# A two-layer transformer step on one core: written order around the layer norms, statistics in halves, last norm's shift as a two-row product

## The chip, the cores and the metric

One core of a Trainium2 chip. The metric is device time in microseconds (us) from launch to end; lower is better. Three runs of the kernel before gave 2600.35, 2598.08 and 2597.52 us (median 2598.08).

## The reference, cut to what matters

Two layers over 256 tokens (g = 0: 128 prompt tokens, g = 1: 128 latent tokens), width 2048. Each layer norm is followed by an adaLN modulation that feeds the next weight product.

```python
def hybrid_layer(x, mods, ...):
    shift1, scale1, gate1, shift2, scale2, gate2 = mods
    h = modulate(x, shift1, scale1)
    q, k, v, hq, hff, hfb, hi, hgt = split_in(h @ w_in_l)
    ...
    mix = jnp.concatenate([att, hg], -1) @ w_o_l
    x = layer_norm(DEEPNORM_ALPHA * x + gate1 * mix, ln_g_l[0], ln_b_l[0])
    ffn = sq_relu_mlp(modulate(x, shift2, scale2), w_up_l, w_down_l)
    x = layer_norm(DEEPNORM_ALPHA * x + gate2 * ffn, ln_g_l[1], ln_b_l[1])
    return x, k, v, s_f, s_b
```

## The kernel before, in words

**Weight stream.** All weights are read once from HBM, in items of 1 MB (two `raw` tiles of 128x1024 f32), loaded by the queue of SyncE (L1310). Ten `raw` buffers hold five items. A *main* item is a block of w_in, w_o, w_up or w_down: ScalarE rounds it to `wh` (L1328), VectorE forms the remainder `wl` (L1329), and TensorE makes three products per block, hi x wh, lo x wh and hi x wl, where `hh`/`hl` are the rounded activations and their remainder. Kind "T" (L445, L447, L448) has the weights stationary and 256 columns moving; kind "N" (L457 to L459) has the activations stationary and 512 columns moving. Four main items (kg = 0 to 3, two or four per part of w_o) make a *unit* with two PSUM banks (for N: g = 0 and g = 1), which a `done` function empties. A *mod* item is a block of w_mod: either four f32 products with two rows of output each on TensorE (L203), or four multiply-adds on VectorE (L266, tile `ma`).

**Order.** `seq` is the written list of items; `put_unit` lays main items and, by the credits RATE and PRATE, mod items between them; `flush` puts out the mod items that must be done. Waiting tasks (attention, scan, plain norm outputs) are stepped in between by `pump`. The order on SyncE and GpSimd is as written; that on TensorE, VectorE and ScalarE is chosen by a list scheduler when the program is built, except inside `manual_schedule`. Each engine then runs its list in order.

**The norms.** There are four: norm 1 (layer 0, behind w_o), norm 2 (layer 0, behind w_down), norm 3 (layer 1, behind w_o) and norm 4 (layer 1, behind w_down, the output). The unit just ahead of a norm I call its *tail*. `add_gated` or `d_down` multiplies each PSUM bank by the gate `G`, adds it to the residual (`Y` or `Z`) and takes `bn_stats` (L891). For norms 1 to 3 `ln_mod` (L933) then aggregates (L909), forms the reciprocal deviation (L621 to L627, two steps of it on ScalarE), normalises each chunk of 512 columns on VectorE (L942), transposes it on TensorE into `pt` (L947), applies scale and shift by feature (`scale_shift`: g = 0 on VectorE L929, g = 1 on ScalarE L931) into `ed`, and splits the result into `hh` (L408, ScalarE) and `hl` (L409, VectorE). One chunk is the activation of one kg of the next unit. After it, `GAP` = 6 mod items are put in. `ln_out` writes the plain output of the norm (times gamma, plus beta, L1013 and L1014) as a task; its rows of gamma and beta are loaded by GpSimd's queue into the two `G` buffers.

**Norm 4** (`ln_last_ordered`): gamma and beta are loaded for all four chunks; two of the eight tiles are finished on GpSimd, one is shared, five take two VectorE instructions each (L974, L998), and each is stored by SyncE.

## Time and profile before

| what | value |
|---|---|
| median of three runs | 2598.08 us |
| the profiled execution, its own time | 2595.31 us |
| its span, first to last instruction | 2593.4 us |
| mean granted TensorE clock | 0.989 |
| busy: VectorE, ScalarE, GpSimd | 1849.1, 1227.5, 105.0 us |
| moved by DMA | 652.77 MB, 252 GB/s in the mean |

Busy time of TensorE counts each matmul with its drain, so two that follow closely overlap; how fast it works is read from the distance of starts. In a timeline a row gives start, duration, engine, line, operation and, in brackets, the idle time before it with what ended it.

### The profile page before, as it was taken

The page shows a single profiled execution, that of the slowest core. Times are in us where ns is not written, and L with a number is a line of the kernel's source. Part 1 is how long each engine was busy: PE and PEld are TensorE (multiplying, and loading weights), DVE is VectorE, ACT ScalarE, POOL GpSimd, SP SyncE. Part 2 cuts the span into 40 slices and gives each one's busy share as a digit, 9 for nine tenths or more (in the row PEclk, how much of TensorE's full clock was granted, in tenths as well). Part 3 has the DMA queues.
Part 4 walks back from the last instruction along what each step waited for, and adds up shares of the span by engine and source line. Part 5 has one row for each costly group of instructions (what it writes and reads, how often), then busy time and mean ns, then how long its engine had stood idle before and what let it go on. Part 6 is the DMA issues. An engine that isn't in the chain of part 4 may idle for free.

```text
span 2593.4 us, 41149 instructions
## 1 busy us (share of the span) xinstructions
PE 2508.7 (97%) x16276; PEld 2150.2 (83%) x16276; DVE 1849.1 (71%) x2332; ACT 1227.5 (47%) x1703; POOL 105.0 (4%) x188
## 2 busy tenths in 40 slices
PE   7999899999999999999999999999899999999996
PEld 4787777768989879879877989788798998998985
DVE  3455778679887777887777788868865565666656
ACT  3434565435545444444435666744544454443542
POOL 2000000000000000000000010001000000000002
PEclk9999999999999999999999999999999999999998
DMA  9889778989987787887878576566576666666663
GB/s 357 271 285 321 268 246 284 325 277 359 315 295 274 267 292 269 285 276 263 288 234 292 193 243 197 193 221 223 187 235 218 212 215 217 217 200 227 204 206 115
DMA packets 192304, 652.77 MB, mean 252 GB/s; under 512 B 22720, under 2 KB 25344, under 8 KB 192112
## 3 DMA queue, kind: packets, MB, share of 16 engines
q1 hardware_dynamic: 177680, 614.56, 69.1%
q0 software_dynamic: 11488, 32.91, 4.3%
q8 instruction: 127, 2.08, 0.3%
q10 hardware_dynamic: 2944, 2.69, 0.3%
q14 instruction: 65, 0.53, 0.1%
HBM read 643.19 MB, written 6.88 MB: 251 GB/s over the span
## 4 chain that ended last, share of the span: by engine, by line
PE 61%; issue 28%; DMA 5%; DVE 4%; ACT 1%; POOL 0%; SPq 0%; POOLq 0%; DVEq 0%; ACTq 0%
PE acc L445 9%; PE acc L447 9%; PE acc L448 9%; PE acc L457 9%; PE acc L459 9%; PE acc L458 9%; DMA raw<-in_w_mod_dram 2%; PE psm L203 2%; DVE wl L1329 1%; PE psm L223 1%; DMA out_nsf_dram<-lf 1%; PE pI L757 1%; PE pX L780 1%; DMA raw<-in_w_in_dram 0%; PE pO L818 0%
## 5 line engine op out<-in xcount | busy, mean ns | idle before, releaser
L1328 ACT CAST wh<-raw 128x1024 fp32r<-128x1024 f32 x784 | 821.7, 1049 | 1065.3 <-PE acc L459 456.2
L1329 DVE TENSOR_TENSOR wl<-raw,wh 128x1024 fp32r<-128x1024 f32 x784 | 953.6, 1222 | 416.1 <-ACT wh L1328 397.1
L445 PE MATMUL acc<-hh,wh 128*128 128x256 f32 x3072 | 878.4, 286 | 3.0 <-DVE q L608 1.7
L448 PE MATMUL acc<-hh,wl 128*128 128x256 f32 x3072 | 871.3, 284 | 5.5 <-DVE wl L1329 5.5
L447 PE MATMUL acc<-hl,wh 128*128 128x256 f32 x3072 | 871.4, 284 | 0.0
L445 PEld LDWEIGHTS acc<-hh,wh 128*128 128x128 f32 x3072 | 589.9, 192 | 40.9 <-issue 31.2
L448 PEld LDWEIGHTS acc<-hh,wl 128*128 128x128 f32 x3072 | 589.9, 192 | 6.5 <-DVE wl L1329 6.5
L447 PEld LDWEIGHTS acc<-hl,wh 128*128 128x128 f32 x3072 | 590.2, 192 | 0.9 <-issue 0.2
L266 DVE SCALAR_TENSOR_TENSOR ma<-raw,stat,ma 128x1024 f32<-128x1024 f32 x300 | 378.6, 1281 | 95.0 <-DMA raw<-in_w_mod_dram 91.2
L458 PE MATMUL acc<-wl,fh 128*128 128x512 f32 x1024 | 399.4, 390 | 4.7 <-DVE wl L1329 4.7
L457 PE MATMUL acc<-wh,fh 128*128 128x512 f32 x1024 | 400.6, 391 | 1.8 <-DVE Z L1241 1.8
L459 PE MATMUL acc<-wh,fl 128*128 128x512 f32 x1024 | 398.9, 390 | 0.0
L457 PEld LDWEIGHTS acc<-wh,fh 128*128 128x128 f32 x1024 | 192.3, 188 | 51.0 <-issue 7.7
L458 PEld LDWEIGHTS acc<-wl,fh 128*128 128x128 f32 x1024 | 192.3, 188 | 45.4 <-DVE wl L1329 6.3
L459 PEld LDWEIGHTS acc<-wh,fl 128*128 128x128 f32 x1024 | 192.3, 188 | 40.0
L458 PE MATMUL acc<-wl,hh 128*128 128x512 f32 x320 | 129.4, 404 | 4.4 <-DVE wl L1329 4.4
L457 PE MATMUL acc<-wh,hh 128*128 128x512 f32 x320 | 131.3, 412 | 2.1 <-ACT hh L408 2.1
L459 PE MATMUL acc<-wh,hl 128*128 128x512 f32 x320 | 127.8, 402 | 0.0
L457 PE MATMUL acc<-wh,mxh 128*128 128x512 f32 x256 | 103.2, 404 | 0.0
L458 PE MATMUL acc<-wl,mxh 128*128 128x512 f32 x256 | 100.1, 392 | 0.0
L459 PE MATMUL acc<-wh,mxl 128*128 128x512 f32 x256 | 100.0, 392 | 0.0
L203 PE MATMUL psm<-raw,stat 128*2 128x512 f32 x640 | 95.0, 596 | 2.4 <-DMA raw<-in_w_mod_dram 2.4
(360 smaller groups left out, 1902.6 us busy)
## 6 DMA issues: line engine op xcount, KB each, us to landing
raw<-in_w_mod_dram SPq DMA_DIRECT2D x384, 512.0 KB
raw<-in_w_up_dram SPq DMA_DIRECT2D x256, 512.0 KB
raw<-in_w_down_dram SPq DMA_DIRECT2D x256, 512.0 KB
raw<-in_w_in_dram SPq DMA_DIRECT2D x208, 512.0 KB
...
```

What stands on the lines that cost most here:

```text
L203: pe.matmul(self.ps[32 * j:32 * j + 2, :], lhsT=stat[:, k, :], rhs=raw[j // 2][:, 512 * (j % 2):512 * (j % 2) + 512], start=k == 0, stop=k ...
L223: pe.matmul(self.ps[32 * j:32 * j + 2, :], lhsT=stat[:, 4 * k + j, :], rhs=raw[j // 2][:, 512 * (j % 2):512 * (j % 2) + 512], start=k == 0 ...
L266: dve.scalar_tensor_tensor(self.acc[g], raw[h], c, self.acc[g], ALU.mult, ALU.add)
L445: pe.matmul(ps, lhsT=w0, rhs=hi[:, k], start=f and k == 0 and m % 2 == 0, stop=False, skip_group_check=True)
L447: pe.matmul(ps, lhsT=w0, rhs=lo[:, k], start=False, stop=False, skip_group_check=True)
L448: pe.matmul(ps, lhsT=w1, rhs=hi[:, k], start=False, stop=e and k == 3 and m % 2 == 1, skip_group_check=True)
L457: pe.matmul(ps, lhsT=hi[:, k, gs], rhs=wh[k], start=f and k == 0, stop=False)
L458: pe.matmul(ps, lhsT=hi[:, k, gs], rhs=wl[k], start=False, stop=False)
L459: pe.matmul(ps, lhsT=lo[:, k, gs], rhs=wh[k], start=False, stop=e and k == 3)
L757: pe.matmul(pI[:, 128 * m:128 * m + 128], lhsT=ke[:, 128 * m:128 * m + 128], rhs=qe[:, 128 * m:128 * m + 128], start=True, stop=True)
L1328: act.copy(wh, r)
L1329: dve.tensor_tensor(wl, r, wh.bitcast(F32), ALU.subtract)
```

## The change

It does these things:

- In the tail unit the g = 1 half of the last kg runs as two halves of 256 columns (`n_tile` with `cols`), and gate, add and `bn_stats` of g = 1 go by halves.
- From the tail's last main item to the end of the next unit, VectorE and ScalarE run in written order (`ordered`). In it the `wh` of two main items is made ahead of the norm (`split(..., False)`), chunk 0 is normalised on two engines (g = 0 ScalarE, g = 1 VectorE), its `hh` is made on ScalarE straight from PSUM while VectorE makes the unrounded copy, and chunk n + 1 is normalised as part of chunk n. The chunks of `ln_mod` now stand between the main items of the next unit.
- No mod items by RATE within the tail; the `flush` ahead of a norm stands before the tail; GAP goes from 6 to 4, and those items stand behind kg = 1 of the next unit.
- The plain outputs of a norm may not be issued before the last `hl` of `ln_mod` (`issue_after`).
- Norm 4: gamma multiplies chunks 0 to 2 already as they are emptied. Then shift: `-mean*rstd*gamma + beta` is made by TensorE as a product with two rows (gamma and beta of a chunk at partitions 32n) into PSUM, one for each of six tiles; VectorE takes one instruction for each of these and two for each tile of chunk 3. GpSimd computes nothing there. The loads for it are put two units earlier: eight single rows and five broadcasts in place of eight broadcasts.

```diff
+                if g == 1 and un.tail:
+                    for h in range(2):
+                        n_tile(un, g, range(4), hi, lo, wh, wl, f, e, slice(256 * h, 256 * h + 256))
+                else:
+                    n_tile(un, g, range(4), hi, lo, wh, wl, f, e)
...
+    def add_gated(key, n, g, ps, gt, first, last, tail):
+
+        for cols in halves(g) if tail else [slice(0, 512)]:
+            t = gt[:, cols]
+            dve.tensor_tensor(t, ps[:, cols], t, ALU.mult)
+            y = yt[key, n, g][:, cols]
+            if first:
+                dve.scalar_tensor_tensor(y, y, ALPHA, t, ALU.mult, ALU.add)
+            else:
+                dve.tensor_tensor(y, y, t, ALU.add)
+            if last and tail:
+                stats(key, n, g, cols.start // 256)
+        if last and not tail:
+            for h in range(len(halves(g))):
+                stats(key, n, g, h)
...
+    def ln_norm(key, n, g):
+        mr, nb = lnst[key]
+        y = yt[key, n, g]
+        if g == 0:
+            act.activation(y, y, AF.Identity, scale=mr[0][1], bias=nb)
+        else:
+            dve.tensor_scalar(y, y, mr[1][0], mr[1][1], ALU.subtract, ALU.mult)
+
+    def ln_open(key):
         mr = ln_stat(key)
+        nb = small(1)
+        dve.scalar_tensor_tensor(nb, mr[0][0], -1.0, mr[0][1], ALU.mult, ALU.mult)
+        lnst[key] = mr, nb
+        for g in range(2):
+            ln_norm(key, 0, g)
+
+    def ln_mod(key, AB, dst, n):
+
+        A, B = (x[:, 4 * n:4 * n + 4] for x in AB)
+        hl = new_act("h")
+        gs = [slice(0, 128), slice(128, 256)]
+        pt, t = {}, {}
+        for g in (1, 0):
+            pt[g] = bank("pt")
+            t[g] = u("ed")
+            for c in range(4):
+                pe.transpose(pt[g][:, 128 * c:128 * c + 128], yt[key, n, g][:, 128 * c:128 * c + 128], K["ident"])
+        if n == 0:
+            for c in range(4):
+                for g in (1, 0):
+                    act.activation(hl[0][:, c, gs[g]], pt[g][:, 128 * c:128 * c + 128], AF.Identity,
+                                   scale=A[:, c, g:g + 1], bias=B[:, c, g:g + 1])
+            ln_norm(key, 1, 1)
+            for c in range(4):
+                cs = slice(128 * c, 128 * c + 128)
+                for g in (1, 0):
+                    dve.tensor_scalar(t[g][:, cs], pt[g][:, cs], A[:, c, g:g + 1], B[:, c, g:g + 1],
+                                      ALU.mult, ALU.add)
+            ln_norm(key, 1, 0)
+        else:
+            for g in (1, 0):
+                scale_shift(t[g], pt[g], A, B, g)
+            for g in (0, 1):
+                act.copy(hl[0][:, :, gs[g]], v3(t[g], 4))
+            if n < 3:
+                for g in (1, 0):
+                    ln_norm(key, n + 1, g)
+        for g in (0, 1):
+            lnend[key] = dve.tensor_tensor(hl[1][:, :, gs[g]], v3(t[g], 4), hl[0][:, :, gs[g]].bitcast(F32),
+                                           ALU.subtract)
+        dst[n] = hl
...
+    def ordered(on):
+
+        if on:
+            region[0] = tc.manual_schedule(engines={mybir.EngineType.DVE, mybir.EngineType.Activation})
+            region[0].__enter__()
+        else:
+            region[0].__exit__(None, None, None)
...
+                side.dma_start(gb[32 * n + i:32 * n + i + 1, :], a[src][li:li + 1, 512 * n:512 * n + 512])
+        lgb["rows"] = gb
         for n in range(4):
-            tag = ("w", "t", "e1", "ed")[n]
-            gt, bt = u(tag), u(tag)
-            side.dma_start(gt, a["lng"][li:li + 1, 512 * n:512 * n + 512].partition_broadcast(128))
-            side.dma_start(bt, a["lnb"][li:li + 1, 512 * n:512 * n + 512].partition_broadcast(128))
-            lgb[li, n] = (gt, bt)
+            lgb["g", n] = rows(("e1", "e1", "ed", "ed")[n], "lng", n)
+        lgb["b", 3] = rows("w", "lnb", 3)
+        mr = u("t", 256)
+        dve.memset(mr, 0.0)
+        dve.memset(mr.rearrange("p (x r) -> p x r", r=32)[:, :, 1], 1.0)
+        lgb["mr"] = mr
...
+        st = ln_stat(key)
+        mr = lgb["mr"]
         for g in range(2):
+            m, r = st[g]
+            cols = mr[:, 128 * g:128 * g + 128].rearrange("p (n r) -> p n r", r=32)[:, :, 0]
+            dve.scalar_tensor_tensor(cols, m.to_broadcast([128, 4]), -1.0, r.to_broadcast([128, 4]),
+                                     ALU.mult, ALU.mult)
+        pt = bank("pt")
+        for g in range(2):
+            pe.transpose(pt[:, 128 * g:128 * g + 128], mr[:, 128 * g:128 * g + 128], K["ident"])
+        cf = u("t", 256)
+        act.copy(cf, pt[:, 0:256])
+        ps = {}
+        for g in range(2):
+            for n in range(3):
+                ps[n, g] = bank("pz")
+                pe.matmul(ps[n, g], lhsT=cf[32 * n:32 * n + 2, 128 * g:128 * g + 128],
+                          rhs=lgb["rows"][32 * n:32 * n + 2, :], start=True, stop=True, tile_position=(32 * n, 0))
+        for g in range(2):
+            y = ys[3, g]
+            dve.scalar_tensor_tensor(y, y, st[g][0], lgb["g", 3], ALU.subtract, ALU.mult)
+            dve.scalar_tensor_tensor(y, y, st[g][1], lgb["b", 3], ALU.mult, ALU.add)
+            store(3, g)
+        for g in range(2):
+            for n in range(3):
+                y = ys[n, g]
+                dve.scalar_tensor_tensor(y, y, st[g][1], ps[n, g], ALU.mult, ALU.add)
+                store(n, g)
...
+                with tc.issue_after(lnend[key].ins):
+                    dve.tensor_tensor(y, y, gt, ALU.mult)
+                    dve.tensor_tensor(y, y, bt, ALU.add)
...
+        opening = closing = False
+        if norm:
+            key, coef, dst = norm[0][:3]
+            opening, closing = un.tail, not un.tail
         for kg in un.groups:
+            if opening and kg == un.groups[-1]:
+                AB = []
+                put_call(drain)
+                put_call(lambda: AB.append(ln_coef(*coef)))
+                put_call(lambda: ordered(True))
+                norm[0] += (AB,)
+            if closing:
+                AB = norm[0][3]
+                if kg == 0:
+                    put_call(lambda: split(main_ahead(at[0], 2), False))
+                    put_call(lambda: ln_open(key))
+                    put_call(lambda: ln_mod(key, AB[0], dst, 0))
+                if kg == 1:
+                    credit[0] += GAP
+                if kg < 3:
+                    put_call(lambda kg=kg: ln_mod(key, AB[0], dst, kg + 1))
+                else:
+                    norm.pop()
             seq.append(("main", Main(un, kg)))
+            if closing and kg == 3:
+                put_call(lambda: ordered(False))
...
+                tail = part == len(PARTS[l]) - 1 and n == 3
+                if tail:
+                    flush((l, 3), (l, 4))
+                    put_norm(k1, (l, 4, 3, 2 * l), h2)
+                put_unit(Unit("N", lambda kg, n=n: a["w_o"][l, n, kg], getM, d_wo(n, part), gr, tail),
+                         0 if tail else RATE[l, "o"], None,
...
-                        t = macc.pop((n, g))
-                        gt = gch.pop((l, 5, n, g, 0))
-                        dve.tensor_tensor(gt, un.ps[g], gt, ALU.mult)
-                        dve.tensor_tensor(t, t, gt, ALU.add)
-                        yt[k2, n, g] = t
-                        stats(k2, n, g)
+                        yt[k2, n, g] = macc.pop((n, g))
+                        add_gated(k2, n, g, un.ps[g], gch.pop((l, 5, n, g, 0)), False, True, un.tail)
+                        if l == L - 1 and n < 3:
+                            y = yt[k2, n, g]
+                            dve.tensor_tensor(y, y, lgb["g", n], ALU.mult)
...
-                    if l == L - 1 and n == 2:
+                    if l == L - 1 and n == 0:
                         put_call(lambda: load_gb(2 * l + 1))
+                tail = sc == 3 and n == 3
+                if tail and l + 1 < L:
+                    flush((l + 1, 0), (l + 1, 1))
+                    put_norm(k2, (l + 1, 1, 0, 2 * l + 1), hcur)
...
-    GAP = 6
+    GAP = 4
...
+    def split(upto, low=True):
+
         while nsplit[0] < min(upto, len(seq)):
             i = nsplit[0]
             issue(i + 1)
             if nd[0] <= i:
-                return
+                break
             it = seq[i]
             if it[0] == "main":
                 m = it[1]
                 m.wh, m.wl = [], []
                 for r in raws.pop(i):
                     wh = whp.tile([128, 1024], F32R, tag="wh", name=nm("wh"))
-                    wl = wlp.tile([128, 1024], F32R, tag="wl", name=nm("wl"))
                     act.copy(wh, r)
-                    dve.tensor_tensor(wl, r, wh.bitcast(F32), ALU.subtract)
                     m.wh += [wh[:, 0:512], wh[:, 512:1024]]
-                    m.wl += [wl[:, 0:512], wl[:, 512:1024]]
-                live[0] -= 2
+                    lows.append((m, wh, r))
+                if low:
+                    split_low()
             nsplit[0] += 1
+        if low:
+            split_low()
+
+    def split_low():
+        for m, wh, r in lows:
+            wl = wlp.tile([128, 1024], F32R, tag="wl", name=nm("wl"))
+            dve.tensor_tensor(wl, r, wh.bitcast(F32), ALU.subtract)
+            m.wl += [wl[:, 0:512], wl[:, 512:1024]]
+            live[0] -= 1
+        lows.clear()
```

**The order on TensorE around norm 1.** Before, at the end of the tail (`psm` rows are mod items, `pt` rows the transposes of a chunk; each mod row is two of the four products of an item):

```order
L459 MATMUL acc_5558<-wh_5543,mxl_5180 128x512
L203 MATMUL psm_5587<-raw_5483,stat 2x512 x2
L203 MATMUL psm_5587<-raw_5485,stat 2x512 x2
L203 MATMUL psm_5587<-raw_5531,stat 2x512 x2
L203 MATMUL psm_5587<-raw_5533,stat 2x512 x2
L203 MATMUL psm_5587<-raw_5547,stat 2x512 x2
L203 MATMUL psm_5587<-raw_5549,stat 2x512 x2
L203 MATMUL psm_5587<-raw_5593,stat 2x512 x2
L203 MATMUL psm_5587<-raw_5595,stat 2x512 x2
L203 MATMUL psm_5587<-raw_5605,stat 2x512
L947 MATMUL pt_5669<-ident_591,Y_4461 128x128 x4
L947 MATMUL pt_5681<-ident_591,Y_4457 128x128 x4
```

Now, at the same place:

```order
L463 MATMUL acc_5561<-wh_5544,mxh_5179 128x256
L465 MATMUL acc_5561<-wl_5548,mxh_5179 128x256
L466 MATMUL acc_5561<-wh_5544,mxl_5180 128x256
L979 MATMUL pt_5677<-ident_591,Y_4461 128x128 x4
L979 MATMUL pt_5683<-ident_591,Y_4457 128x128 x4
L979 MATMUL pt_5711<-ident_591,Y_4664 128x128 x4
L450 MATMUL acc_5745<-hh_5675,wh_5597 128x256
L450 MATMUL acc_5758<-hh_5675,wh_5597 128x256
L979 MATMUL pt_5717<-ident_591,Y_4660 128x128 x4
L452 MATMUL acc_5745<-hl_5676,wh_5597 128x256
```

The mod items between the tail and the first transposes are gone (before there are 24 of their products, six items, between the tail and the first main product of w_up); 16 transposes in place of 24 stand ahead of the first product that needs `hl`. At norm 2 the list now has 16 mod products in this place in place of 24; at norm 3 there were and are none.

**The order on VectorE at norm 3.** Before, from the tail's g = 0 bank on (`wl` rows belong to the weights of the next unit):

```order
L896 TENSOR_TENSOR G_17825<-acc_17841,G_17825 128x512
L901 TENSOR_TENSOR Y_17458<-Y_17458,G_17825 128x512
L891 BN_STATS bs_17651<-Y_17458 128x6
L909 BN_AGGR s_17914<-bs_17651 128x2
L1329 TENSOR_TENSOR wl_18040<-raw_17707,wh_18039 128x1024
L896 TENSOR_TENSOR G_17827<-acc_17848,G_17827 128x512
L1329 TENSOR_TENSOR wl_18044<-raw_17709,wh_18043 128x1024
L901 TENSOR_TENSOR Y_17462<-Y_17462,G_17827 128x512
L891 BN_STATS bs_17655<-Y_17462 128x6
L909 BN_AGGR s_17914<-bs_17655 128x2
```

Now:

```order
L911 TENSOR_TENSOR G_17866<-acc_17892,G_17866 128x512
L916 TENSOR_TENSOR Y_17472<-Y_17472,G_17866 128x512
L905 BN_STATS bs_17673<-Y_17472 128x6
L911 TENSOR_TENSOR G_17868<-acc_17899,G_17868 128x256
L916 TENSOR_TENSOR Y_17476<-Y_17476,G_17868 128x256
L905 BN_STATS bs_17677<-Y_17476 128x6
L911 TENSOR_TENSOR G_17868<-acc_17899,G_17868 128x256
L916 TENSOR_TENSOR Y_17476<-Y_17476,G_17868 128x256
L905 BN_STATS bs_17677<-Y_17476 128x6
L927 BN_AGGR s_17996<-bs_17673 128x2
L927 BN_AGGR s_17996<-bs_17677 128x2
```

The two `wl` subtractions are no longer among the statistics of g = 1; these go by halves.

**The plain outputs on VectorE behind norm 1** (`Y` rows, times gamma and then plus beta). Before:

```order
L1013 TENSOR_TENSOR Y_4457<-Y_4457,G_6629 128x512
L1013 TENSOR_TENSOR Y_4461<-Y_4461,G_6629 128x512
L1329 TENSOR_TENSOR wl_6160<-raw_6013,wh_6159 128x1024
L1014 TENSOR_TENSOR Y_4457<-Y_4457,G_6630 128x512
L1329 TENSOR_TENSOR wl_6164<-raw_6015,wh_6163 128x1024
L266 SCALAR_TENSOR_TENSOR ma_6007<-raw_6025,stat,ma_6007 128x1024
L266 SCALAR_TENSOR_TENSOR ma_6008<-raw_6025,stat,ma_6008 128x1024
L266 SCALAR_TENSOR_TENSOR ma_6007<-raw_6027,stat,ma_6007 128x1024
L1329 TENSOR_TENSOR wl_6228<-raw_6097,wh_6227 128x1024
L266 SCALAR_TENSOR_TENSOR ma_6008<-raw_6027,stat,ma_6008 128x1024
L1329 TENSOR_TENSOR wl_6232<-raw_6099,wh_6231 128x1024
L1014 TENSOR_TENSOR Y_4461<-Y_4461,G_6630 128x512
```

Now:

```order
L1001 TENSOR_TENSOR hl_5918<-ed_5920,hh_5917 128x4x128
L1091 TENSOR_TENSOR Y_4457<-Y_4457,G_6626 128x512
L1091 TENSOR_TENSOR Y_4461<-Y_4461,G_6626 128x512
L1092 TENSOR_TENSOR Y_4457<-Y_4457,G_6627 128x512
L1092 TENSOR_TENSOR Y_4461<-Y_4461,G_6627 128x512
L1450 TENSOR_TENSOR wl_5947<-raw_5889,wh_5943 128x1024
L1091 TENSOR_TENSOR Y_4660<-Y_4660,G_6986 128x512
L1450 TENSOR_TENSOR wl_5949<-raw_5891,wh_5945 128x1024
```

They now stand directly behind the last `hl`, and the first instruction of the second chunk (`G_6986`, a `G` buffer that has to be loaded again) stands between the two `wl` of kg = 3.

## Rows read from the trace of the kernel before

**Rows 1.** Page of the profile, part 1: busy time of each engine.

```profile
PE 2508.7 (97%) x16276; PEld 2150.2 (83%) x16276; DVE 1849.1 (71%) x2332; ACT 1227.5 (47%) x1703; POOL 105.0 (4%) x188
```

**Rows 2.** Stretches, TensorE: us, busy (instructions), granted clock, DMA share, GB/s.

```profile
600.00:602.00 2.00, 2.00 (x12) 1.00 1.03 410
...
1382.00:1384.00 2.00, 2.00 (x6) 0.53 0.87 277
...
1838.00:1840.00 2.00, 0.00 (x0) 0.88 1.00 391
...
1846.00:1848.00 2.00, 1.70 (x14) 0.92 0.00 0
...
2576.00:2578.00 2.00, 0.00 (x0) 0.70 0.00 0
```

**Rows 3.** Lines of TensorE, 590.7 to 602.4 us: count, busy, mean ns, idle before.

```profile
L203 PE MATMUL psm<-raw,stat 128*2 128x512 f32 x48 | 8.0, 592 | 0.9 <-DMA raw<-in_w_mod_dram 0.9
```

**Rows 4.** Timeline around norm 1, TensorE, VectorE and ScalarE in turn.

```profile
590.52 0.39 PE L459 MATMUL acc<-wh,mxl 128*128 128x512 f32 x1
...
602.46 0.48 PE L445 MATMUL acc<-hh,wh 128*128 128x256 f32 x2
...
608.18 1.03 PE L947 MATMUL pt<-ident,Y 128*128 128x128 f32 x8
608.97 0.36 PE L448 MATMUL acc<-hh,wl 128*128 128x256 f32 x1
609.26 1.04 PE L203 MATMUL psm<-raw,stat 128*2 128x512 f32 x8
610.23 0.39 PE L445 MATMUL acc<-hh,wh 128*128 128x256 f32 x1
...
590.95 0.69 DVE L896 TENSOR_TENSOR G<-acc,G 128x512 f32<-128x512 f32 x1 [0.28 <-PE acc L459]
...
593.43 0.17 DVE L621 TENSOR_SCALAR s<-s 128x2 f32<-128x2 f32 x1
...
594.90 2.37 DVE L942 TENSOR_SCALAR Y<-Y,s,s 128x512 f32<-128x512 f32 x5
...
604.36 1.29 DVE L409 TENSOR_TENSOR hl<-ed,hh 128x512 fp32r<-128x512 f32 x2
...
602.17 1.50 ACT L931 ACTIVATE ed<-pt,B,A 128x128 f32<-128x128 f32 x4
```

**Rows 5.** Timeline around norm 2, TensorE.

```profile
1359.94 0.39 PE L459 MATMUL acc<-wh,fl 128*128 128x512 f32 x1
...
1371.79 0.48 PE L457 MATMUL acc<-wh,hh 128*128 128x512 f32 x1
...
1381.01 0.50 PE L458 MATMUL acc<-wl,hh 128*128 128x512 f32 x1 [2.12 <-DVE wl L1329]
...
1382.81 0.63 PE L459 MATMUL acc<-wh,hl 128*128 128x512 f32 x1
```

**Rows 6.** Timeline around norm 3, TensorE.

```profile
1836.41 0.39 PE L459 MATMUL acc<-wh,mxl 128*128 128x512 f32 x1
...
1849.18 0.36 PE L447 MATMUL acc<-hl,wh 128*128 128x256 f32 x1
```

**Rows 7.** Timeline of norm 4, TensorE and VectorE.

```profile
2571.80 0.39 PE L459 MATMUL acc<-wh,fl 128*128 128x512 f32 x1
...
2577.76 1.64 DVE L998 SCALAR_TENSOR_TENSOR Z<-Z,s,t 128x512 f32<-128x512 f32 x1
...
2588.22 0.75 DVE L998 SCALAR_TENSOR_TENSOR Z<-Z,s,ed 128x512 f32<-128x512 f32 x1
```

**Rows 8.** Line 563, f32 products of 512 columns: durations ns min/median/max.

```profile
L563 PE MATMUL pr<-q,rot x8: 590/592/596, 488.7 to 1769.6; 128*128 128x512 f32 x8
```

**Rows 9.** Timeline behind norm 3, VectorE and TensorE.

```profile
1876.70 0.69 DVE L1013 TENSOR_TENSOR Y<-Y,G 128x512 f32<-128x512 f32 x1 [4.58 <-DMA G<-in_lng_dram]
...
1879.77 0.38 PE L448 MATMUL acc<-hh,wl 128*128 128x256 f32 x1 [1.13 <-DVE wl L1329]
```

119 lines of the change are left out of this document (40 added, 79 removed).

## The prediction

> **What bounds the kernel now.** I read part 1 of the page first: TensorE is busy 97% of the span, VectorE, the next, 71% [rows 1]. So time is lost where TensorE stands still, and an edit counts by the TensorE idle time that it adds or takes away. A mod item is work that must be done somewhere: moved, it costs nothing in itself, but it fills a hole or leaves one open. Next come the stretches, for clock and DMA load at the norms [rows 2], and the lines of TensorE at norm 1 [rows 3]; then the timeline of each norm, from the start M of the tail's last matmul to the first matmul behind it [rows 4 to 7].
>
> At norm 1 M is 590.52 and the first main product 602.46, a gap of 11.94 us. The reader is to see that it isn't empty. Eight mod rows take 0.97, 0.121 each [rows 4], so the 48 of the gap [rows 3] take 5.8; eight transposes take 0.79, 0.1 each [rows 4], and the 24 ahead of the first product that needs `hl` take 2.4. The last matmul itself takes 0.23 (its 0.39 holds a tail of 0.16). Idle: 11.94 - 5.8 - 2.4 - 0.23 = 3.5 us.
>
> Norm 2 has the same work in a gap of 11.85 (1359.94 to 1371.79): 3.4 idle. Behind it TensorE waits 2.1 for a `wl`, and then eight matmuls start 0.43 apart, each 0.63 long, in place of 0.23 apart and 0.39 long, 1.6 lost [rows 5]; the granted clock reads 0.53, near 1.2 GHz [rows 2]. In all 7.1.
>
> Norm 3 has no mod items in its gap, which is 12.77 long (1836.41 to 1849.18) [rows 6]: less 28 transposes (2.8), 0.23 and two short products (0.24), 9.5 idle.
>
> **Norms 1 and 3: the new chain.** VectorE starts 0.43 behind M (590.95) [rows 4]. A gate multiplication of 512 columns takes 0.69 there; for a half I take 0.45, between its half, 0.36 with some fixed cost, and the whole, 0.72. Three such (the last half's gate, add, statistics) are 1.35, and two aggregates 0.6, an estimate from the 2.48 between 590.95 and 593.43, in which three whole operations stand besides. So M + 2.4. From there to the normalisation 1.47 (593.43 to 594.90), plus 0.2 for the new `nb`: M + 4.05. Half a microsecond for a tile (five in 2.37) makes M + 4.6, eight transposes and the way there M + 5.7. Then ScalarE forms `hh` in eight pieces: four took 1.50, so 0.35 each and a longer last one, 2.9, M + 8.7 with the hand-overs. Two `hl` take 1.3 (1.29) [rows 4]: M + 10.1. Near norm 3 the clock reads 0.88 two microseconds behind M and 0.92 when transposes run again [rows 2]; for eight transposes at half clock I add 0.8: M + 10.9. Ends: 9.8 (halves at 0.36, full clock), and 11.7 (halves at 0.72).
>
> In it TensorE has 16 transposes (1.6) and 0.4 of short products, the last matmul among them: 8.9 idle. The lists show it: no mod item stands there any more. **Norm 1: 8.9 - 3.5 = +5.4. Norm 3: 8.9 - 9.5 = -0.6.** The main costs of norm 1 that the change takes away (normalisation of later chunks out of the way, `wh` made ahead) are in the shorter chain already; the six mod items are done before the tail and behind kg = 1, where VectorE and the DMA have other work.
>
> **Norm 2.** Here 16 mod products stand in the gap (32 rows, 3.9), 16 transposes (1.6) and four matmuls (0.9). They keep TensorE at work, so the chain ends at M + 10.1; with 0.1 for the last matmul, 3.6 is idle. The `wl` of two items is made behind the norm now, before its products need it, so I let the 2.1 and the 1.6 go. **3.6 - 7.1 = -3.5**; if both stay, +0.2.
>
> **Plain outputs.** Behind norm 1 the first instruction on the second chunk stands between two `wl` of kg = 3, and needs a `G` buffer that GpSimd's queue loads again. What waits behind it on VectorE is the other `wl`, and behind that TensorE. The nearest rows are behind norm 3: VectorE waited 4.58 for such a load, and 1.13 of it reached TensorE [rows 9]. Between 0 and 4.6; I take **+0.7**, near the lower of the two, since the products of kg = 2 and the mod items stand ahead.
>
> **Norm 4.** M is 2571.80. Before, the last instruction of VectorE ends at 2588.97, M + 17.17, and the span (2593.4) at M + 21.6, 4.43 later for the store. While GpSimd computes, VectorE's instruction takes 1.64, alone 0.75 [rows 7]. Now GpSimd computes nothing. Statistics are done at M + 3.9 (as above without `nb`); chunk 3 takes four instructions and the six other tiles one each: 10 x 0.75 = 7.5, M + 11.4, 5.75 earlier than before, if no product is late. A product is an f32 one of 512 columns in two passes; a pass lasts 0.59 [rows 8] with the tail of 0.16, so 0.43, a product 0.86. Columns, transposes and copy end near M + 5. One after another at full clock, product i is ready at M + 5.2 + 0.86 i, the sixth at M + 10.3, and VectorE wants it at M + 10.65: no wait. At half clock, as the stretch that reads 0.70 in this place suggests [rows 2], the sixth is ready at M + 15.5 and VectorE ends at M + 16.3: only -0.8. I take a wait of 0.6 near the first end, because the products run while VectorE works on chunk 3: **-5.2**, between -5.75 and -0.8.
>
> No run here shows products that use 2 rows of the array each at other rows. The Trainium skill, TensorEngine Tiling (Array Packing), Tiling Modes, states that different tiles can work in parallel and that a change of tiling mode drains the engine; by it three products would go side by side, and even the half clock would leave no wait, -5.75. The nearest rows show four mod products that share the array by columns done in 0.97 [rows 4], which agrees for columns alone.
>
> **At nothing.** Three gamma multiplications for each g (six times 0.7, 4 us) lie on VectorE (71% busy) under units of TensorE; without that cover 4 us. The 13 loads of norm 4 stand on GpSimd's queue two units earlier than the 8 before; their buffers (`e1`, `ed`, `w`, `t`) are small, and TensorE's weights come by SyncE's queue. The halved matmuls in four tails: up to 0.15 each, +0.5 at the upper end.
>
> **Sum:** 5.4 - 0.6 - 3.5 + 0.7 - 5.2 = **-3.2**. All durations are of the profiled execution, 2595.31, which the sum takes to 2592.1; the median of the runs is 2598.08, 2.77 above it, and the sum against it gives **2594.9 us**. A measurement of this kernel can tell some 0.2%, 5.2 us, from no change: faster is below 2592.9, slower above 2603.3.
>
> **The rivals.**
>
> *B, the order pays more.* The outputs no longer stand ahead of `wl`: the 0.7 is not lost and the 1.13 behind norm 3 [rows 9] goes; the products of norm 4 are never late (0.6); at norms 1 and 3 the chain is at its lower end (9.8 in place of 10.9, 2.2 for both). -3.2 - 0.7 - 1.1 - 0.6 - 2.2 = -7.8: 2590.3. For it: these waits are in the trace. Against it: a new instruction with a load stands between two `wl` at norm 1.
>
> *C, TensorE goes slow in the open gap.* Norm 1 gets 9 us without mod products and restarts as norm 2 did before, 1.6 lost [rows 5]; at norm 4 the six products run one after another at half clock and decide the end (4.4 less gain, from the point at which a product takes longer than VectorE's 0.75 and the lead of four). -3.2 + 1.6 + 4.4 = +2.8: 2600.9. For it: 0.88 and 0.70 in stretches in which TensorE did nothing, and 0.53 behind norm 2 [rows 2]. Against it: the transposes, and at norm 3 the clock was near full again at 1846 [rows 2]. The Trainium skill, TensorE: Matmul & The Clock Gate, Part 1, puts it that the default state is throttled and activity releases the throttle; it speaks against an open gap, and the 0.53 and 0.70 agree.
>
> *D, slower: the weight stream.* Mod items hold their raw buffers until they are used. Those taken from the gap of norm 1 now stand behind kg = 1, two chunks of `ln_mod` later; I work out that up to four of the five items' buffers are held until about M + 25, so that nothing can be loaded from about M + 5 to M + 14, some 9 us. At that place the DMA share is 1.03, 410 GB/s [rows 2], and TensorE waits 0.9 for a mod block [rows 3]. If the stage is bound by its loads, each microsecond without one is lost: from the point at which the buffers' lead no longer covers 9 us, up to +9. -3.2 + 9 = +5.8: 2603.9. Against it: over the whole span 252 GB/s are moved on average, so the stream catches up in the next stage, and a lead of five items (5 MB, 13 us at 391 to 410 GB/s) may cover it.
>
> **How the numbers follow.** The forecast has 0.45: its terms come from rows, and its two largest are of opposite signs. B 0.28: all its parts are waits that the trace shows. C 0.14, D 0.13: each needs more than its cause. Faster: nearly all of B and a lower part of the forecast, 0.33; slower: D and a bit of C, 0.14; the rest, 0.53, within 0.2%. The range goes from 2588 (B, less 0.3 if the chain of norm 2 is at its lower end too, and 2 us for the spread of the runs, 2597.5 to 2600.4) to 2603 (C whole, the lower part of D).
>
> **What would show it.** Right: gaps from M to the first product with `hl` of about 11 us at norms 1 to 3, with 9, 4 and 9 idle; no wait for `wl` behind norm 2; at norm 4 ten instructions of 0.75 and the span's end at M + 16.4. B shows as no wait for G on VectorE behind norms 1 and 3; C as granted clocks near 0.5 behind norm 1 and at the six products, VectorE waiting for these; D as a DMA share near zero around norm 1 and TensorE waiting for weights after it. The prediction is wrong if the sum is moved by a place that none of these names: a wait in the stages between the norms, where the new list on VectorE or ScalarE also moves instructions.

## The result, and the profile after

The changed kernel takes 2622.64 us (median of five runs, 2612.89 to 2625.89), the kernel before 2597.52 (five runs): ratio 1.0092, 95% interval 1.0074 to 1.0110. By the ratio it is **24 us slower** (25 by the medians); 2594.9 was forecast, with 2603 as the upper end. The profiled execution is the one of 2622.64 us.

Part 1 of the page of the changed kernel. TensorE is still the engine that is busy 97% [rows 1]; VectorE and ScalarE are busy for about as long as before (1849.1 and 1227.5 us there).

```profile
span 2620.9 us, 41314 instructions
...
PE 2530.3 (97%) x16338; PEld 2163.9 (83%) x16338; DVE 1847.7 (71%) x2366; ACT 1234.2 (47%) x1719; POOL 99.4 (4%) x188
```

Where the time went is seen from the last matmul of each tail, M, in both timelines ([rows 4 to 7] for before, the fences below for after), and from the first product of the w_o stage of layer 1:

| to | before, us | after, us | stretch longer by |
|---|---|---|---|
| M of norm 1 | 590.52 | 591.87 | +1.4 |
| M of norm 2 | 1359.94 | 1371.08 | +9.8 |
| first product of w_o, layer 1 | 1736.82 | 1753.49 | +5.5 |
| M of norm 3 | 1836.41 | 1865.39 | +12.3 |
| M of norm 4 | 2571.80 | 2605.01 | +4.2 |
| end of the span | 2593.4 | 2620.9 | -5.7 |

Only the last line went as forecast. The first says nothing: the kernels of this study that are written like the changed one up to norm 1 have this M anywhere from 587.7 to 593.9. The w_o stage is steadier: 111.9 us in three kernels with seven mod items in it (after, chunk0, c0nog), 99.6 to 100.4 in five with none (before, norm4_alone, n4_gap8, cover3, together). Its first product, before and after, and M of norm 4 after:

```profile
1736.82 0.50 PE L457 MATMUL acc<-wh,mxh 128*128 128x512 f32 x1
...
1753.49 0.50 PE L463 MATMUL acc<-wh,mxh 128*128 128x512 f32 x1
...
2605.01 0.28 PE L466 MATMUL acc<-wh,fl 128*128 128x256 f32 x1
```

The timeline of TensorE at norm 1 (start, duration, engine, line, operation, idle time before it):

```profile
591.87 0.28 PE L466 MATMUL acc<-wh,mxl 128*128 128x256 f32 x1
597.45 2.79 PE L979 MATMUL pt<-ident,Y 128*128 128x128 f32 x12 [5.30 <-DVE Y L959]
...
602.73 1.11 PE L979 MATMUL pt<-ident,Y 128*128 128x128 f32 x4 [1.99 <-ACT Y L957]
605.72 0.58 PE L452 MATMUL acc<-hl,wh 128*128 128x256 f32 x1 [1.88 <-DVE hl L1001]
606.10 0.42 PE L453 MATMUL acc<-hh,wl 128*128 128x256 f32 x1
...
608.88 0.35 PE L452 MATMUL acc<-hl,wh 128*128 128x256 f32 x1
```

M to the first product with `hl` is 13.85 us (591.87 to 605.72), where 10.9 was worked out. VectorE and ScalarE there (timeline):

```profile
592.19 0.42 DVE L911 TENSOR_TENSOR G<-acc,G 128x256 f32<-128x256 f32 x1 [0.72 <-PE acc L466]
...
593.45 0.41 DVE L911 TENSOR_TENSOR G<-acc,G 128x256 f32<-128x256 f32 x1
...
595.22 0.17 DVE L629 TENSOR_SCALAR s<-s 128x2 f32<-128x2 f32 x1
...
596.76 1.00 DVE L959 TENSOR_SCALAR Y<-Y,s,s 128x512 f32<-128x512 f32 x2
601.66 2.67 DVE L989 TENSOR_SCALAR ed<-pt,A,B 128x128 f32<-128x128 f32 x8 [3.90 <-ACT hh L983]
604.37 1.29 DVE L1001 TENSOR_TENSOR hl<-ed,hh 128x512 fp32r<-128x512 f32 x2
...
598.58 0.46 ACT L983 ACTIVATE hh<-pt,B,A 128x128 fp32r<-128x128 f32 x1 [0.88 <-PE pt L979]
599.43 2.55 ACT L983 ACTIVATE hh<-pt,B,A 128x128 fp32r<-128x128 f32 x7 [0.40 <-PE pt L979]
```

The halves of the tail gained nothing. The last product of the first half starts at 590.43, but VectorE, idle for 0.72 us, begins with that half only at 592.19, when the last product of the second half is done. Both halves lie in one PSUM bank, which is the likely reason; it was not tried. So all six half operations stand behind M, 2.6 us of them, and the reciprocal deviation (L629) begins at M + 3.35; before, with whole operations, it began at M + 2.91 (593.43) [rows 4]. The transposes begin at M + 5.6 and the eighth is done at M + 7.5, where 5.7 was worked out, or 6.5 at half clock.

Then VectorE waits 3.90 us for ScalarE's `hh` and only behind them makes its eight unrounded copies from the same two PSUM banks: ScalarE's `hh` end at 601.98, and VectorE's 2.67 us follow almost whole. Norms 2 and 3 show the same, with waits of 4.61 and 3.90, and 14.0 and 13.85 from M to `hl`:

```profile
1371.08 0.28 PE L466 MATMUL acc<-wh,fl 128*128 128x256 f32 x1
...
1376.28 1.17 PE L204 MATMUL psm<-raw,stat 128*2 128x512 f32 x2 [2.23 <-DMA raw<-in_w_mod_dram]
...
1385.07 0.50 PE L466 MATMUL acc<-wh,hl 128*128 128x512 f32 x1 [1.72 <-DVE hl L1001]
...
1865.39 0.28 PE L466 MATMUL acc<-wh,mxl 128*128 128x256 f32 x1
...
1879.24 0.58 PE L452 MATMUL acc<-hl,wh 128*128 128x256 f32 x1 [1.87 <-DVE hl L1001]
```

The stretches around norm 1 (us, busy time of PE, PEld, DVE, ACT, POOL, granted clock, DMA share, GB/s):

```profile
590.00:600.00 10.00, 4.70 (x31) 4.43 (x30) 6.15 (x19) 4.24 (x8) 1.08 (x2) 0.77 0.63 236
600.00:610.00 10.00, 6.13 (x31) 5.44 (x30) 8.07 (x19) 5.92 (x14) 0.00 (x0) 0.55 0.00 0
...
630.00:640.00 10.00, 7.57 (x51) 7.37 (x50) 6.40 (x6) 6.79 (x9) 0.00 (x0) 0.83 1.03 391
```

Two things that only rivals foretold: the clock is at 0.55, near 1.2 GHz, where the products begin again (0.21 us from start to start until 608.88, 0.12 afterwards), and no byte is loaded for ten microseconds. The wait further on, VectorE at 633 us:

```profile
633.60 0.69 DVE L1091 TENSOR_TENSOR Y<-Y,G 128x512 f32<-128x512 f32 x1 [3.81 <-DMA G<-in_lng_dram]
634.21 1.22 DVE L1450 TENSOR_TENSOR wl<-raw,wh 128x1024 fp32r<-128x1024 f32 x1
```

The plain output waits 3.81 us for its `G`, the second `wl` behind it is late, and TensorE stands still for 2.43 us (from 632.77 plus its 0.28 to 635.48).

Then the mod items. Before, none stood in the w_o stage of layer 1; the tile `psm` there now, 1753 to 1866 us (count, durations, first and last start):

```profile
L204 PE MATMUL psm<-raw,stat x56: 591/592/592, 1759.8 to 1853.3; 128*2 128x512 f32 x56
```

Seven items (56 rows). Two fewer in each gap and three fewer in the tails left them over; six are put there one by one by the credit RATE of that stage, which before found none left, and the last by the flush ahead of the tail. From the start of their rows to the next matmul they take 9.6 us. Five stand whole and take 0.97 each, as in a row of items [rows 4]; two are broken up by transposes into five blocks of two to six rows, and each block takes 0.95 or 0.96. The whole stage is 12.3 us longer.

Norm 4, VectorE, and the products on TensorE (12 rows: six products of two passes each):

```profile
2609.48 0.75 DVE L1069 SCALAR_TENSOR_TENSOR Z<-Z,s,ed 128x512 f32<-128x512 f32 x1
...
2612.80 2.72 DVE L1075 SCALAR_TENSOR_TENSOR Z<-Z,s,pz 128x512 f32<-128x512 f32 x4 [0.34 <-PE pz L1065]
2615.71 1.41 DVE L1075 SCALAR_TENSOR_TENSOR Z<-Z,s,pz 128x512 f32<-128x512 f32 x2 [0.19 <-PE pz L1065]
...
2610.70 5.64 PE L1065 MATMUL pz<-w,t 2*128 2x512 f32 x12 [0.46 <-ACT t L1060]
```

Ten instructions of 0.75 and 0.53 of waiting: VectorE ends at 2617.12, M + 12.1, and the span at M + 15.9. Before these were 17.2 and 21.6 [rows 7]; so 5.1 of the 5.7 us are VectorE's; the rest is a shorter time from its end to that of the span, 3.8 us in place of 4.4.

### The profile page after: what moved, and what is told of

It reads as the page before. It is cut to its first block, busy times and chain, and to the rows that moved or that the text cites. A ratio compares the mean times of both kernels' runs of the same rounds, so it can differ in the third digit from the quotient of the medians.

```text
span 2620.9 us, 41314 instructions
## 1 busy us (share of the span) xinstructions
PE 2530.3 (97%) x16338; PEld 2163.9 (83%) x16338; DVE 1847.7 (71%) x2366; ACT 1234.2 (47%) x1719; POOL 99.4 (4%) x188
## 4 chain that ended last, share of the span: by engine, by line
PE 62%; issue 27%; DVE 5%; DMA 4%; ACT 2%; POOL 0%; SPq 0%; ACTq 0%; DVEq 0%; POOLq 0%
PE acc L450 9%; PE acc L453 9%; PE acc L452 9%; PE acc L463 9%; PE acc L465 9%; PE acc L466 9%; PE psm L204 2%; DMA raw<-in_w_mod_dram 2%; DVE wl L1450 1%; PE psm L224 1%; DMA out_nsf_dram<-lf 1%; ACT wh L1438 1%; DVE ma L267 1%; PE pI L765 1%; PE pO L826 1%
## 5 line engine op out<-in xcount | busy, mean ns | idle before, releaser
L465 PE MATMUL acc<-wl,fh 128*128 128x512 f32 (+1 forms) x1032 | 401.6, 389 | 7.2 <-DVE wl L1450 7.2
L463 PE MATMUL acc<-wh,fh 128*128 128x512 f32 (+1 forms) x1032 | 401.8, 389 | 0.0
L466 PE MATMUL acc<-wh,fl 128*128 128x512 f32 (+1 forms) x1032 | 400.7, 388 | 0.0
L463 PE MATMUL acc<-wh,mxh 128*128 128x512 f32 (+1 forms) x264 | 105.1, 398 | 0.3 <-ACT mxh L409 0.3
L466 PE MATMUL acc<-wh,mxl 128*128 128x512 f32 (+1 forms) x264 | 101.3, 385 | 0.0
L465 PE MATMUL acc<-wl,mxh 128*128 128x512 f32 (+1 forms) x264 | 101.2, 384 | 0.0
```

The costliest lines, as they stand in the source:

```text
L463: pe.matmul(ps, lhsT=hi[:, k, gs], rhs=wh[k][:, cols], start=f and k == 0, stop=False, skip_group_check=skip)
L465: pe.matmul(ps, lhsT=hi[:, k, gs], rhs=wl[k][:, cols], start=False, stop=False, skip_group_check=skip)
L466: pe.matmul(ps, lhsT=lo[:, k, gs], rhs=wh[k][:, cols], start=False, stop=e and k == 3, skip_group_check=skip)
```

## The experiments

Ratios are against the kernel before, in runs on the same chip; 0.001 is 2.6 us. Differences of two experiments are differences of their ratios, some of them from different chips; by the two intervals each carries 6 to 8 us of uncertainty. Where less is at stake, the trace has to decide.

**norm4_alone.** Before, with `load_gb`, `ln_last_ordered` and the gamma multiplication of the change, and nothing else.

```diff
                         stats(k2, n, g)
+                        if l == L - 1 and n < 3:
+                            dve.tensor_tensor(t, t, lgb["g", n], ALU.mult)
...
-                    if l == L - 1 and n == 2:
+                    if l == L - 1 and n == 0:
                         put_call(lambda: load_gb(2 * l + 1))
```

> Before, with norm 4 of the change alone (the two-row products, gamma multiplied as chunks 0 to 2 are emptied, the loads two units earlier). In the changed kernel the time from the last matmul of the tail to the end of the span is 15.9 us, before 21.6. Theory A (that gain stands by itself, all losses lie at norms 1 to 3): 5.7 us faster than before. Rival B (the gamma multiplications and the early loads cost something in the w_down stage): 0 to 3 us faster.

Measured: 2593.51 us, ratio 0.9981 (0.9963 to 0.9999), 4.9 us faster, with 0.3 and 9.6 as the ends of the interval: the time alone does not part theory A from rival B. The trace speaks for A: M of norm 4 stands at 2571.63, where it stood before (2571.80), so the w_down stage lost nothing, and the span (2587.5) ends 15.9 behind it. That tail has no halves, so they gave nothing at norm 4 either. It is the only kernel of the study whose interval lies below 1, if only just.

```profile
2571.63 0.39 PE L459 MATMUL acc<-wh,fl 128*128 128x512 f32 x1
```

**warm.** The changed kernel with products that nobody reads.

```diff
+    def warm(n):
+        for _ in range(n):
+            pe.matmul(bank("pw"), lhsT=K["ident"], rhs=K["rmask"], start=True, stop=True)
...
+                    put_call(lambda: warm(6))
                     put_call(lambda: ln_open(key))
                     put_call(lambda: ln_mod(key, AB[0], dst, 0))
+                    put_call(lambda: warm(2))
```

> The changed kernel with eight products in the gap of each norm 1 to 3 that nobody reads (identity by a constant tile of 512 columns, six behind the tail and two behind the transposes of chunk 0). They change no chain and cover no work. Theory A (a part of the loss is TensorE's clock: at norms 1 and 3 it is at half for 13.7 us each, in which it works for about 7.7 us): 3 to 4 us less at each of these two norms and 1.7 at 636 us, 6 to 9 us faster than the changed kernel, granted clock near 1.0 behind norms 1 and 3. Rival B (the loss is all waiting for the chain and for weights): within 2 us of the changed kernel, or slower by the 1 us that the products stand in the way of transposes.

Measured: 2619.09 us, ratio 1.0075 (1.0051 to 1.0100), against 1.0092: some 4 us less, less than theory A gave and within the uncertainty. The trace shows the mechanism: the same stretches around norm 1 now read

```profile
590.00:600.00 10.00, 9.85 (x47) 6.45 (x46) 7.78 (x20) 3.21 (x5) 1.08 (x2) 1.00 0.75 286
600.00:610.00 10.00, 6.72 (x35) 5.27 (x33) 6.92 (x18) 6.94 (x16) 0.00 (x0) 0.86 0.00 0
```

0.86 in place of 0.55. M to `hl` is 13.0 in place of 13.85 us. The clock still falls once (behind the second wait of the gap), so this prices a part of it; by this run most of the 24 us is not clock.

**cover.** Six mod items back in the gap, ahead of the statistics.

```diff
+                    put_mods(6)
                     put_call(lambda: ln_open(key))
...
-    GAP = 4
+    GAP = 0
```

> The changed kernel with six mod items back in the gap of norms 1 and 2, ahead of the statistics, and none behind kg = 1. Theory A (the loss at norm 1 is cover: work of 5.8 us now stands elsewhere, at 1.4 us for an item by itself in place of 0.97, and the clock falls): gap of norm 1 as long as now (13.9) with 5.8 of it filled, 9 to 13 us faster than the changed kernel in all. Rival B (the loss is the weight stream that stands still while mod items hold raw buffers): only the 2.4 us wait for wl at 633 us goes, and the clock stretch behind it, 3 to 4 us faster. Rival C (the chain alone matters): no change within 2 us.

Measured: 2629.6 us, ratio 1.0124 (1.0098 to 1.0150): 8 us slower still, at the edge of the uncertainty, which none of the three foretold. TensorE's timeline there:

```profile
597.00 6.89 PE L204 MATMUL psm<-raw,stat 128*2 128x512 f32 x44 [3.32 <-issue]
603.82 0.55 PE L979 MATMUL pt<-ident,Y 128*128 128x128 f32 x3
```

The first item needs its PSUM bank zeroed, and that instruction stands behind the statistics in VectorE's written order; so the items started 3.3 us late and ran for 6.9 us, into the time at which the transposes were ready; and the list also put the transposes of chunk 2 ahead of the first main product. The run says nothing on the worth of cover, only that written order and mod items get in each other's way.

**chunk0.** Chunk 0 like the others (`if n < 0` in place of `if n == 0` in `ln_mod`).

> The changed kernel with chunk 0 treated like chunks 1 to 3: g = 0 scaled on VectorE and g = 1 on ScalarE, then hh copied on ScalarE, then hl. Theory A (in the change VectorE starts its copy of chunk 0 only when ScalarE is done with all eight hh, 3.9 us of waiting, so the two copies stand one behind the other): from the first transposes to the first product with hl 8.3 us now, 4.5 to 5 then, 3.3 us less at each of norms 1 to 3, 8 to 12 us faster than the changed kernel. Rival B (hh straight from PSUM pays, the wait is of no account since products with hh run in it): 0 to 4 us slower.

Measured: 2612.8 us, ratio 1.0055 (1.0037 to 1.0072) against 1.0092: 9.6 us less. Theory A. M to `hl` is now 11.6, 10.6 and 11.6 us at norms 1 to 3, in all 7.8 less. At norm 1 (TensorE):

```profile
587.68 0.28 PE L466 MATMUL acc<-wh,mxl 128*128 128x256 f32 x1
...
599.31 0.56 PE L452 MATMUL acc<-hl,wh 128*128 128x256 f32 x1
```

The waits of VectorE behind the norm, of the changed kernel (592 to 608 us) and of chunk0 (587 to 605):

```profile
DVE ed L989 <- ACT hh L983: 3.9, 1, 3.9
```

```profile
DVE ed L947 <- PE pt L979: 3.2, 2, 2.1
```

The wait for ScalarE is gone. Of the edits tried this one gives back the most.

**cover5t.** The cover by itself on top of chunk0, with the two faults of the run cover mended (`issue_after` holds the transposes of chunks 2 and 3 behind the products of an earlier item).

```diff
                     flush((l, 3), (l, 4))
+                    put_mods(1)
...
+                    put_mods(5)
                     put_call(lambda: ln_open(key))
...
-    GAP = 4
+    GAP = 0
```

> The kernel chunk0 with five mod items in the gap of norms 1 and 2 and none behind kg = 1; one mod item, with the zeroing of its PSUM bank, is put ahead of the tail of norm 1, and the transposes of chunks 2 and 3 are held behind the products of the item two before them, so that nothing of the mod items waits for VectorE and the chain is that of chunk0. Theory A (cover: the gap has 5.3 us of idle time ahead of its first transposes, mod items fill it and would cost 1.0 to 1.4 us each elsewhere): 6 to 10 us faster than chunk0, transposes at the same distance from the last matmul of the tail (5.4 us) to within 1 us. Rival B (the items hold the transposes back, as the six of the run cover did by 5 us): within 3 us of chunk0 or slower.

Measured: 2613.51 us, ratio 1.0058 (1.0036 to 1.0079): as chunk0. The items ran at once and the transposes were not held back, but (waits of TensorE, 588 to 660 us)

```profile
PE acc L452 <- ACT wh L1443: 4.3, 1, 4.3
```

Five items fill all ten raw buffers, so the weights of the next unit are not there when `wh` should be made ahead, and ScalarE's written order then has them behind chunk 1. What the cover gave was taken by this wait.

**cover3** and **cover5w** ease that in two ways. cover3: three items in the gap (`put_mods(3)`) and GAP = 4. cover5w:

```diff
-                    put_call(lambda: split(main_ahead(at[0], 2), False))
+                    put_mods(5)
                     put_call(lambda: ln_open(key))
                     put_call(lambda: ln_mod(key, AB[0], dst, 0))
+                    put_call(lambda: split(main_ahead(at[0], 2), False))
...
-    GAP = 4
+    GAP = 3
```

> As cover5t, but with three mod items in the gap and four more behind kg = 1: three leave raw buffers for the first two items of the next unit, so that their wh is made ahead of the chain, as in chunk0 (in cover5t ScalarE made it behind chunk 1, and TensorE waited 4.3 us for it). Theory A (cover): 3 us of the idle time ahead of the transposes filled, no wait for wh, five or six items fewer in the w_o stage of layer 1 at 1.4 us each, less time at half clock: 8 to 12 us faster than chunk0. Rival B (the items cost as much in the gap as elsewhere, since they take the place of weight loads): within 3 us of chunk0.

> As cover5t, with wh of the next two items made right behind hh of chunk 0 in the written order of ScalarE, in place of behind chunk 1, and three more mod items behind kg = 1. Theory A (cover, and the 4.3 us wait for wh in cover5t came from the written order): the wait falls to 1 to 2 us, 8 to 13 us faster than chunk0. Rival B (wh is late because its weights cannot be loaded while five mod items hold all raw buffers): the wait for wh stays at 3 us or more, within 3 us of cover5t.

Measured: cover3 2609.57 us, ratio 1.0031 (1.0016 to 1.0046); cover5w 2608.96, ratio 1.0031 (1.0019 to 1.0044). Both 6 us less than chunk0, with an uncertainty of 6: between theory A's 8 us and rival B's 3, and neither is ruled out. In the trace of cover3 there is no mod row left in the w_o stage of layer 1, and that stage is 12.1 us shorter than in chunk0. But the stretch from M of norm 1 to M of norm 2 is 13.7 us longer (785.3 against 771.6), so in these two executions all of it is given back in layer 0. What TensorE waited for most, 590 to 720 us, and its timeline at norm 1 (M is 589.38):

```profile
PE psm L204 <- DMA raw<-in_w_mod_dram: 6.1, 2, 3.1
```

```profile
600.32 3.10 PE L204 MATMUL psm<-raw,stat 128*2 128x512 f32 x8 [2.98 <-DMA raw<-in_w_mod_dram]
603.36 1.82 PE L982 MATMUL pt<-ident,Y 128*128 128x128 f32 x8
```

The items wait for their loads and hold the transposes back to M + 14.0, and the first product with `hl` to M + 21.1: here the mechanism is rival B's. Of cover5w only times are used.

**before_gap0.** The price of cover in the kernel before: `GAP = 0` in place of 6, one line.

> The kernel before with GAP = 0: the six mod items behind norm 1, and the six behind norm 2, come later by RATE or by the flush, nothing else changes. Theory A (cover: these items cost nothing in a gap in which TensorE has to wait anyway, and 1.0 to 1.4 us each elsewhere; the clock falls in the empty gap): 10 to 18 us slower than before. Rival B (TensorE idles often enough elsewhere that the items find other holes): 0 to 4 us slower.

Measured: 2621.87 us, ratio 1.0085 (1.0065 to 1.0105), 22 us slower, above the upper end of theory A. TensorE's longest wait from 585 to 700 us (in total, times, longest), and VectorE behind norm 1, where M is 590.95:

```profile
PE pt L947 <- DVE Y L942: 10.1, 1, 10.1
```

```profile
595.31 1.28 DVE L266 SCALAR_TENSOR_TENSOR ma<-raw,stat,ma 128x1024 f32<-128x1024 f32 x1 [2.39 <-DMA raw<-in_w_mod_dram]
```

and the tile `psm` in the w_o stage of layer 1:

```profile
L203 PE MATMUL psm<-raw,stat x96: 591/592/593, 1765.0 to 1865.5; 128*2 128x512 f32 x96
```

Twelve items leave the gaps of norms 1 and 2, and twelve (96 rows) turn up in the w_o stage of layer 1. This one line makes the kernel before as slow as the changed one, but not by cover alone: with it the list of VectorE changes too. A multiply-add that waits 2.39 us for its load now stands between the gate and the statistics of norm 1, the first transposes begin at M + 11.4 in place of 6.5, and the stretch from norm 1 to norm 2 is 16.5 us longer, though it holds six items fewer. So the 22 us are not the price of twelve items out of place.

**gap0.** chunk0 with `GAP = 0` in place of 4.

> The kernel chunk0 with GAP = 0: no mod items behind kg = 1, so none of them holds raw buffers while the gap lasts; they come later by RATE or by the flush ahead of norm 3. Theory A (the weight stream that stands still for some 15 us around norm 1 costs time afterwards): DMA share above 0.5 from 600 to 620 us, TensorE waits less behind norm 1, 3 to 6 us faster than chunk0. Rival B (the stop is made good by the lead of the stream; the waits behind norm 1 are those of the plain outputs): within 2 us of chunk0.

Measured: 2625.15 us, ratio 1.0100 (1.0080 to 1.0119), 12 us slower than chunk0; neither theory had that. The eight items land ahead of norm 3 too (tile `psm`, 1735 to 1880 us), all in the flush in a row, as the stretch shows:

```profile
L204 PE MATMUL psm<-raw,stat x120: 591/592/1061, 1745.7 to 1855.8; 128*2 128x512 f32 x120
```

```profile
1840.00:1860.00 20.00, 13.61 (x71) 2.10 (x63) 3.70 (x14) 3.37 (x4) 0.54 (x1) 0.91 0.98 362
```

The row of mod items is bound by its loads here: DMA share 0.98 and TensorE busy for 13.6 of 20 us. The DMA share from 590 us on is 0.29, 0.30 and 0.35 in three stretches of 10 us, not above 0.5 as theory A wanted. So items behind kg = 1 were not the trouble, and an item that comes too late costs more than its TensorE time.

**c0nog.** chunk0 with gamma and beta of the plain outputs loaded once.

```diff
-            gt, bt = u("G"), u("G")
+            if n == 0:
+                gt, bt = u("G"), u("G")
...
```

> The kernel chunk0 with gamma and beta of a plain output loaded for chunk 0 alone and used for all four chunks, so the plain outputs of chunks 1 to 3 are not the reference's: no load of a G buffer stands between two wl any more. Theory A (the 2.1 us that TensorE waits for wl behind norm 1, and the 3.4 us at half clock behind it, come from the wait of VectorE for G; 0.9 us behind norm 3 too): 3 to 5 us faster than chunk0. Rival B (the second wl is late because its weights are late): within 1.5 us of chunk0, with the same wait for wl.

Measured: 2609.14 us, ratio 1.0042 (1.0027 to 1.0057), some 3 us less than chunk0, within the uncertainty, so the trace has to tell. The wait of TensorE for `wl`, 585 to 660 us, of chunk0 and of c0nog:

```profile
PE acc L453 <- DVE wl L1450: 2.1, 1, 2.1
```

```profile
PE acc L453 <- DVE wl L1451: 0.4, 1, 0.4
```

Behind norm 1 the wait is the plain output's: theory A there. (It is gone in gap0 too, where the loads of `G` are as they were; so more than one edit takes it away.) The wait behind norm 3 (0.9) stayed.

**n4_gap8.** norm4_alone with `GAP = 8` in place of 6.

> The kernel norm4_alone with GAP = 8: two more mod items in the gaps of norms 1 and 2, of which 3.5 and 3.4 us were idle before. Theory A (an item in the gap is free, elsewhere it costs 1.0 to 1.4 us): 3 to 6 us faster than norm4_alone, some 2588 us. Rival B (the list of TensorE puts them ahead of the transposes and they hold the chain back): within 2 us of norm4_alone or slower.

Measured: 2603.91 us, ratio 1.0012 (0.9995 to 1.0029), 8 us slower than norm4_alone: neither as forecast nor by rival B's mechanism. TensorE's and VectorE's waits, 592 to 720 us, and a stretch:

```profile
PE acc L448 <- DVE wl L1345: 4.9, 5, 2.2
...
DVE Y L1027 <- DMA G<-in_lng_dram: 7.5, 2, 4.3
```

```profile
600.00:610.00 10.00, 10.00 (x73) 6.92 (x73) 8.16 (x20) 7.49 (x18) 0.00 (x0) 1.00 1.02 406
```

In norm4_alone there is neither wait from 592 to 720 us. M to `hl` is as long as there at norm 1 (13.2 us), so the chain is not held back; plain outputs that wait for their `G` now stand ahead of some of these `wl` on VectorE. The DMA is full from 600 to 610 us, but just as full in norm4_alone (share 1.02, 408 GB/s), so that alone does not make the difference. Whether `G` is late by the load of two more items, or the new list only asks for it earlier, was not tried.

**together.** cover3 with the loads of c0nog left out and, at norm 3 alone, the unread products of warm.

> cover3, with gamma and beta of the plain outputs loaded for chunk 0 alone (as in c0nog; the plain outputs of chunks 1 to 3 are not the reference's), and with the eight unread products of the run warm in the gap of norm 3 alone, in which there are no mod items. Theory A (serial copies, cover, plain outputs and clock are separate parts that add up): against before 1.0031 less 0.0013 less some 0.0008, 1.000 to 1.002. Rival B (each part taken away lets the same weight stream become the bound, so that the last two give nothing): 1.003 or more.

Measured: 2599.08 us, ratio 1.0009 (0.9992 to 1.0026). Theory A: the parts add up. With loads left out that the outputs need, the changed kernel is back at the time of before, with norm 4's gain in it; so some 7 us of losses (1.0009 against 0.9981) are still in it. In its trace the stretch from norm 1 to norm 2 (770.7 us) and the w_o stage (99.8) are within 2 us of norm4_alone's (769.1 and 99.6); what is longer is the stretch from M of norm 2 to that stage, 385.5 against 375.9.

## Why the prediction was wrong

Point by point, by its own terms (their sum was -3.2; measured 24 us slower by the ratio, 27.3 by the two profiled executions).

- **Norm 4, -5.2: right.** -5.7 in the trace, 4.9 us faster as a kernel of its own. In part this is luck: chunk 3 begins at M + 4.5 in place of 3.9, since the halves gave nothing, but the ten instructions overlap a little (7.1 us in place of 7.5), and some 0.6 came back at the end of the span. The reason for the small wait was another than supposed, too: the clock was at half, as in rows 2, but products ran side by side (last section).
- **The chain of norms 1 to 3, M + 10.9: mis-sized, in two terms.** One is "Three such (the last half's gate, add, statistics) are 1.35". It let the first half be done before M; the trace has all six half operations behind M, and the statistics end at M + 3.3 in place of 2.4. The other is "Then ScalarE forms `hh` in eight pieces ... Two `hl` take 1.3". It let VectorE's copy of chunk 0 run beside ScalarE's. The order of VectorE shows the copies, but not that they wait for the other engine's; the trace shows 3.90 us of waiting. ScalarE's `hh` end at M + 10.1, where 9.5 was worked out with half clock, and the first product with `hl` starts 3.7 behind them in place of 1.4. M + 13.85 in place of 10.9, at three norms; the run chunk0 gives 9.6 us back, and its 11.6 is what is left with the first fault in it.
- **"Moved, it costs nothing in itself": the premise that failed.** I counted the hole that the mod items leave at norm 1 and not where they land. GAP 4 in place of 6 and none by RATE in the tails leave seven items over for the w_o stage of layer 1, where TensorE has no hole: that stage is 12.3 us longer, 1.8 an item, and in cover3, with none there, 12.1 shorter than in chunk0. It is the largest part of the loss that the table shows.
- **Norm 1, +5.4 and +0.7.** Gap 13.85, less 1.6 for transposes and 0.4 of short products: 11.9 idle or slow, against 3.5, so +8.4. Behind it 1.5 for products at half clock, 2.4 for the wait on the plain output (the +0.7, whose upper end was 4.6) and 1.7 for 3.4 us at half clock after that. Together some +14; the stretch to norm 2 holds four mod items fewer (17, before 21), some 4 us of work, which leaves about the +9.8 of the table.
- **Norm 2, -3.5: wrong sign.** I let the waits behind it go and kept the gap short. From the last four w_down units ahead of it to the first "T" unit behind it, by starts of matmuls, 134.7 us in place of 131.8, with two mod items fewer in it. The gap is 14.0 us; a mod row waits 2.23 for its load there, and 4.87 us of multiply-adds, which the new order of VectorE shows behind kg = 1, delay chunk 2.
- **Norm 3, -0.6.** The gap is 13.85 in place of 12.77, and the products behind it start at half clock.
- **Rival B, 0.28: wrong.** The plain outputs made a wait at norm 1 in place of removing one.
- **Rival C, 0.14: its first half right.** The restarts at norms 1 and 3 are slow, and the price for norm 1, 1.6, was of the right size; TensorE kept at full clock (warm) gave some 4 us, within the uncertainty. Its second half, norm 4, did not come. The Trainium skill, TensorE: Matmul & The Clock Gate, Part 1, has throttled as the default state; the 0.55 agrees.
- **Rival D, 0.13: right in what it saw, wrong in the price.** The stream did stop (DMA share 0.00 for 10 us). That mod items with their buffers stop it is not shown: with none put behind kg = 1 (gap0) the share stays near 0.3 for 30 us, and nothing was gained. The wait of TensorE at 633 us was for the plain output's `G` and not for weights (c0nog).

So the loss that weighed most was taken as free, and neither wait of VectorE at a PSUM bank, the halves' and the one for `hh`, was in any rival. Two things are not settled. What makes the remaining 7 us, which the trace of together has between norm 2 and the w_o stage of layer 1, is not known; it is not the halved products, since the w_o stage of that kernel has them and is 99.8 us long. And the price of an item out of place is 1.4 us by TensorE's rows, 1.8 by the length of the stage and 1.5 from gap0 (12 us, eight items); how much of the difference is clock was not measured by itself.
